# An attention kernel: a planned order of work, and some exponentials computed on VectorE

## The chip, the cores and the metric

The kernel runs on one core of a Trainium2 chip. The metric is the device time of one execution in microseconds; lower is better. The core's engines each run their own queue in order: TensorE (PE in the profile; PEld is its weight load), VectorE (DVE), ScalarE (ACT), GpSimd (POOL) and SyncE (SP), which here issues the transfers between HBM and the core's memory SBUF. TensorE writes to PSUM, eight banks of 2 KB in each partition.

## The reference

Plain attention over 8 batches and 8 heads, 512 queries and keys, 64 dimensions, in fp32:

```python
scale = 1.0 / np.sqrt(q.shape[-1])
scores = np.einsum('bhqd,bhkd->bhqk', q, k) * scale
scores = scores - scores.max(axis=-1, keepdims=True)
attn = np.exp(scores)
attn = attn / attn.sum(axis=-1, keepdims=True)
return np.einsum('bhqk,bhkd->bhqd', attn, v).astype(np.float32)
```

The inputs are normal random numbers. The kernel does not subtract the maximum: it takes the exponential of the scaled scores, and the sum by which it divides comes out of the last product as a 65th column.

## The kernel before

**Tiles.** Two heads make a pair; there are 32 pairs, g = 0 to 31. A pair's queries, keys and values are loaded by SyncE as three tiles of 128 x 512 fp32 (`load`, line 79), cast to fp16 by GpSimd (`cast_v` line 88, `cast_qk` line 95), and queries and keys are turned by TensorE, four 128 x 128 transposes each (`transposes`, line 108), into a PSUM tile that VectorE copies to SBUF (line 109). After that the two heads of a pair lie one above the other, 64 partitions each.

**Scores.** A score block is one chunk of 128 keys of one head against all 512 queries: one matmul with 64 partitions in (line 118). Two blocks make a group, m = 0 to 128; the last two groups have one block each. For most pairs a group has the same chunk of both heads, so a pair has four groups, one for each chunk. A group's scores fill two PSUM banks, `st`, of which there are three pairs; ScalarE reads all 1024 columns and writes the exponentials to SBUF as fp16, `pt` (line 126).

**Values.** When a head's four blocks have their exponentials, 16 small matmuls multiply them with the values, four for each of four parts of the queries (`values`, line 158). The values have a column of ones, so the 65th column of `o` is the sum. VectorE takes its reciprocal (line 136) and multiplies (line 137); that is `normalise`. SyncE stores the pair once both its heads are done.

**Order.** The order on every engine is that of the program text (`manual_schedule`). It is written out by hand: `fill[m]` (lines 229 to 240) lists which transposes and which value products come behind the scores of group m. The values of a head come some six groups behind its scores. Each product's evacuation by VectorE stands right behind it. At the first group of each pair, loads for six pairs ahead and casts for three and two pairs ahead are issued. PSUM outside `st` has two banks: `ps_o` for the products, `ps_t` for the transposes, each with one buffer.

**Head.** `first_loads` and `first_transposes` bring pair 0 in by halves and end with the scores of groups 0 and 1.

Of the kernel before, what the change touches and what calls it, by code (L numbers as in the profile page):

```python
# [7 lines left out]

FP32 = mybir.dt.float32
FP16 = mybir.dt.float16  # L10

EXP = mybir.ActivationFunctionType.Exp
AluOp = mybir.AluOpType


@with_exitstack
def kernel(
# [7 lines left out]
    nc = tc.nc  # L25
# [34 lines left out]
    zeros = cpool.tile([P, S], FP16, name="zeros")  # L60
# [5 lines left out]
    blocks = {}  # L66
    os = {}
    obs = {}

    def source(src, g):  # L70
        b, h = g // ppb, 2 * (g % ppb)
# [26 lines left out]
            )  # L98
        qkp[g] = t

    def transposes(g, n, pool=ps_t, tag="tp"):
        if g >= NP:
            return
        if n == 1:
            tqk[g] = tpool.tile([P, 2, S], FP16, tag="tqk", name=f"tqk_{g}")
        tp = pool.tile([P, NI, P], FP16, tag=tag, name=f"tp_{g}_{n}")
        for i in range(NI):
            nc.tensor.transpose(tp[:, i, :], qkp[g][:, n, i, :], ident)  # L108
        nc.vector.tensor_copy(out=tqk[g][:, n, :], in_=tp.rearrange("p i c -> p (i c)"))  # L109

    def scores(m):
        grp = groups[m]
        size = len(grp)
        st = ps_st.tile([P, 2, S], FP32, tag="st", name=f"st_{m}")
        pt = ppool.tile([P, 2, S], FP16, tag="pt", name=f"pt_{m}")
        for x, (g, c, h) in enumerate(grp):
            po = 64 * h
            nc.tensor.matmul(  # L118
                st[:, x, :],
                tqk[g][po : po + 64, 1, c * P : (c + 1) * P],  # L120
                tqk[g][po : po + 64, 0, :],
                start=True,
                stop=True,
            )
            blocks[(g, c, h)] = pt[:, x, :]
        nc.scalar.activation(  # L126
            out=pt[:, 0:size, :], in_=st[:, 0:size, :], func=EXP, scale=scale
        )

    def normalise(g, h):  # L130
        o = os.pop((g, h))
        if h == 0:
# [3 lines left out]
        nc.vector.reciprocal(out=rc[:, :, :], in_=o[:, :, D : D + 1])  # L136
        nc.vector.tensor_tensor(  # L137
            out=ob[:, h],
            in0=o[:, :, 0:D],
            in1=rc[:, :, :].broadcast_to([P, NI, D]),  # L140
            op=AluOp.mult,
        )
        if g == LAST:
            nc.sync.dma_start(out=source(out, g)[:, h], in_=ob[:, h])
        elif h == 1:
            nc.sync.dma_start(out=source(out, g), in_=ob[:, :, :, :])

    def values(g, h, part):


        last = g == LAST and h == 1
        if part == 0:
            pool, tag = (ps_t, "tp") if g >= LAST - 1 and h == 1 else (ps_o, "o")
            os[(g, h)] = pool.tile([P, NI, D + 1], FP32, tag=tag, name=f"o_{g}_{h}")
        o = os[(g, h)]
        for x in range(NI):
            c, qc = (part, x) if last else (x, part)
            nc.tensor.matmul(  # L158
                o[:, qc, :],
                blocks[(g, c, h)][:, qc * P : (qc + 1) * P],  # L160
                vps[g % NV][:, h, c, :],
                start=(c == 0 and (qc == 0 or not last)),
                stop=(c == NI - 1),
                skip_group_check=last,
            )
        if part == NI - 1:
            normalise(g, h)

    def first_loads():
        tk = load_tile(0, "k")  # L170
        tq = load_tile(0, "q")
# [4 lines left out]
    def first_transposes():  # L176
        tk, tq = raw[0]["k"], raw[0]["q"]
        tqk[0] = tpool.tile([P, 2, S], FP16, tag="tqk", name="tqk_0")
        halves = []
        for h in range(2):  # L180
            t = cpool.tile([P, 2, NI, P], FP16, name=f"qkp_0_{h}")
            nc.gpsimd.memset(t[:, :, :, 64 * (1 - h) : 64 * (1 - h) + 64], 0.0)
            halves.append(t)
        for h in range(2):
            t, s = halves[h], slice(64 * h, 64 * h + 64)
            if h == 0:
                nc.vector.tensor_copy(out=t[:, 1, 0:2, s], in_=tk[:, h, 0:2])  # L187
                nc.vector.tensor_copy(out=t[:, 0, 0:2, s], in_=tq[:, h, 0:2])
                nc.scalar.copy(t[:, 0, 2:4, s], tq[:, h, 2:4])  # L189
                nc.gpsimd.tensor_copy(out=t[:, 1, 2:4, s], in_=tk[:, h, 2:4])  # L190
# [3 lines left out]
        pk = ps_t.tile([P, NI, P], FP16, tag="tp", name="tp_0_k_0")  # L194
        pq = ps_o.tile([P, NI, P], FP16, tag="o", name="tp_0_q_0")
        pk2 = ps_st.tile([P, 2, P], FP16, tag="st", name="tp_0_k2_0")

        def transpose(dst, h, n, i):
            nc.tensor.transpose(dst, halves[h][:, n, i, :], ident)  # L199

        def evacuate(h, n, c0, c1, src):
            s = slice(64 * h, 64 * h + 64)
            nc.vector.tensor_copy(  # L203
                out=tqk[0][s, n, P * c0 : P * c1], in_=src[s].rearrange("p i c -> p (i c)")
            )
# [10 lines left out]
        pk = ps_t.tile([P, NI, P], FP16, tag="tp", name="tp_0_k_1")  # L216
# [4 lines left out]
        pq = ps_o.tile([P, NI, P], FP16, tag="o", name="tp_0_q_1")  # L221
# [7 lines left out]
    fill = [[] for _ in range(M)]  # L229
    for g in range(1, NP):  # L230
        kq = {1: (3, 3), 2: (4, 5)}.get(g, (4 * g - 5, 4 * g - 3))
        fill[kq[0]].append((transposes, (g, 1)))
        fill[kq[1]].append((transposes, (g, 0, ps_o, "o") if g == 1 else (g, 0)))
    for g in range(NP):
        for h in range(2):
            m = 4 * g + 6 + 2 * h
            if (g, h) == (LAST - 1, 1):
                m -= 1
            m = min(m, M - 1)
            fill[m] += [(values, (g, h, part)) for part in range(NI)]  # L240

    with tc.manual_schedule():
        first_loads()
        load(1, "kq")
        load(0, "v")
        for g in range(2, 6):
            load(g, "kq")
            load(g - 1, "v")
        nc.vector.memset(zeros[:, :], 0.0)  # L249
        make_identity(nc, ident)  # L250
        for n in range(NV):
            nc.gpsimd.memset(vps[n][:, :, :, D : D + 1], 1.0)
# [8 lines left out]
        for m in range(M):  # L261
            g, x = divmod(m, 4)
            if x == 0:
                load(g + 6, "kq")
                if g + 5 < NP:
                    load(g + 5, "v")
                cast_qk(g + 3)
                if g + 2 < NP:
                    cast_v(g + 2)
            if m >= 2:  # L270
                scores(m)
            for what, args in fill[m]:
                what(*args)


# [28 lines left out]
```

## Time and profile before

| | |
|---|---|
| median of 3 runs | 129.64 us (129.14 to 130.58) |
| the profiled execution | 129.37 us |
| its span, first to last instruction | 127.5 us |
| ScalarE busy | 119.1 us, 93% |
| TensorE busy | 111.7 us, 88% |
| VectorE busy | 67.5 us, 53% |
| GpSimd busy | 58.3 us, 46% |

Busy shares are of the span. TensorE's matmuls are pipelined and their ends are modelled, so its share does not say how near it is to its limit. A line of a group reads: line, engine, operation, tile written and tile read, their shapes, how many; busy time of all and the mean of one in ns; the engine's idle time ahead of them and what ended it. ScalarE's instructions overlap, so the mean of one is longer than its share of the busy time. In the timeline, times are the start and the length in us.

### The profile page before, as it was taken

The page shows a single profiled execution, that of the slowest core. Times are in us where ns is not written, and L with a number is a line of the kernel's source. Part 1 is how long each engine was busy: PE and PEld are TensorE (multiplying, and loading weights), DVE is VectorE, ACT ScalarE, POOL GpSimd, SP SyncE. Part 2 cuts the span into 40 slices and gives each one's busy share as a digit, 9 for nine tenths or more (in the row PEclk, how much of TensorE's full clock was granted, in tenths as well). Part 3 has the DMA queues.
Part 4 walks back from the last instruction along what each step waited for, and adds up shares of the span by engine and source line. Part 5 has one row for each costly group of instructions (what it writes and reads, how often), then busy time and mean ns, then how long its engine had stood idle before and what let it go on. Part 6 is the DMA issues. An engine that isn't in the chain of part 4 may idle for free.

```text
span 127.5 us, 4004 instructions
## 1 busy us (share of the span) xinstructions
PE 111.7 (88%) x1550; PEld 69.6 (55%) x1550; DVE 67.5 (53%) x198; ACT 119.1 (93%) x131; POOL 58.3 (46%) x111
## 2 busy tenths in 40 slices
PE   6989989889988998898889888988898899888980
PEld 2435656656565655565556555655566565655450
DVE  0535654565456555645665565556555654565161
ACT  4199999999999999999999999999999999999970
POOL 5487858655555533345554333555543347000000
PEclk9999999999999999999999999999999999999996
DMA  3999999999999999988989979989899522222042
GB/s 132 270 352 351 349 351 349 378 370 379 381 348 299 344 373 372 339 272 276 296 248 345 290 249 299 317 275 278 295 306 291 165 85 82 87 82 82 21 133 98
DMA packets 34883, 33.82 MB, mean 265 GB/s; under 512 B 2096, under 2 KB 34864, under 8 KB 34864
## 3 DMA queue, kind: packets, MB, share of 16 engines
q1 hardware_dynamic: 34576, 33.30, 80.6%
q8 instruction: 12, 0.20, 0.7%
q10 hardware_dynamic: 288, 0.26, 0.6%
q14 instruction: 7, 0.06, 0.2%
HBM read 25.17 MB, written 8.39 MB: 263 GB/s over the span
## 4 chain that ended last, share of the span: by engine, by line
ACT 67%; issue 20%; PE 9%; DVE 1%
ACT pt L126 67%; PE st L118 3%; PE o L158 2%; PE warm L255 2%; PE tp L108 1%; PE tp_k L199 1%; PE tp_q L199 0%; DVE ob L137 0%; DVE zeros L249 0%; DVE rc L136 0%
## 5 line engine op out<-in xcount | busy, mean ns | idle before, releaser
L126 ACT ACTIVATE pt<-st 128x1024 f16<-128x1024 f32 x129 | 117.5, 1729 | 2.6 <-PE st L118 2.6
L118 PE MATMUL st<-tqk 64*128 64x512 f16 x256 | 52.0, 384 | 10.7 <-ACT pt L126 10.0
L158 PEld LDWEIGHTS <-pt 128*128 128x128 f16 x1024 | 36.0, 98 | 15.0 <-DVE tqk L109 12.5
L158 PE MATMUL o<-vp,pt 128*128 128x65 f16 x1024 | 43.8, 194 | 0.2 <-ACT pt L126 0.2
L95 POOL CAST qkp<-k 128x512 f16<-128x512 f32 x31 | 19.0, 613 | 44.6 <-issue 34.8
L136 DVE RECIPROCAL rc<-o 128x4 f32<-128x4 f32 x64 | 11.7, 182 | 47.1 <-PE o L158 47.1
L118 PEld LDWEIGHTS <-tqk 64*128 64x128 f16 x256 | 17.4, 93 | 21.3 <-issue 9.5
L137 DVE TENSOR_TENSOR ob<-o,rc 128x256 f32<-128x256 f32 x64 | 27.2, 424 | 2.2
L109 DVE COPY tqk<-tp 128x512 f16<-128x512 f16 x62 | 26.2, 425 | 3.3 <-PE tp L108 2.7
L108 PE MATMUL tp<-ident,qkp 128*128 128x128 f16 x248 | 24.4, 222 | 0.2 <-POOL vp L88 0.2
L108 PEld LDWEIGHTS <-qkp 128*128 128x128 f16 x248 | 14.1, 97 | 14.2 <-issue 7.8
L88 POOL CAST vp<-v 128x512 f16<-128x512 f32 x32 | 19.7, 616 | 1.2
L95 POOL CAST qkp<-q 128x512 f16<-128x512 f32 x31 | 19.0, 614 | 1.4 <-DMA q<-in_q_dram 0.9
L255 PE MATMUL warm<-zeros 128*128 128x512 f16 x6 | 2.7, 630 | 1.2 <-DVE zeros L249 1.2
L189 ACT ACT_TABLE_LOAD x1 | 1.3, 1283 | 1.7 <-PEq L288 1.7
L199 PEld LDWEIGHTS <-qkp 128*128 128x128 f16 x16 | 1.3, 124 | 1.5 <-issue 1.5
L255 PEld LDWEIGHTS <-zeros 128*128 128x128 f16 x6 | 0.7, 138 | 2.3 <-DVE zeros L249 1.2
L187 DVE CAST qkp<-k 128x128 f16<-128x128 f32 x1 | 0.2, 227 | 2.3 <-DMA k<-in_k_dram 2.3
L203 DVE COPY tqk<-tp_q 64x512 f16<-64x512 f16 x2 | 0.8, 422 | 0.9 <-PE tp_q L199 0.7
L199 PE MATMUL tp_k<-ident,qkp 128*128 128x128 f16 x8 | 1.2, 305 | 0.0
L203 DVE COPY tqk<-tp_k 64x256 f16<-64x256 f16 (+1 forms) x3 | 1.0, 328 | 0.4 <-PE tp_k L199 0.3
L199 PE MATMUL tp_q<-ident,qkp 128*128 128x128 f16 x8 | 1.0, 266 | 0.0
(14 smaller groups left out, 4.2 us busy)
## 6 DMA issues: line engine op xcount, KB each, us to landing
v<-in_v_dram SPq DMA_DIRECT2D x32, 256.0 KB, 5.4
k<-in_k_dram SPq DMA_DIRECT2D x31, 256.0 KB, 5.1
q<-in_q_dram SPq DMA_DIRECT2D x31, 256.0 KB, 5.3
out_dram<-ob SPq DMA_DIRECT2D x31, 256.0 KB, 3.7
k<-in_k_dram ACTq DMA_DIRECT2D x2, 128.0 KB, 2.8
q<-in_q_dram SPq DMA_DIRECT2D x2, 128.0 KB, 2.6
out_dram<-ob SPq DMA_DIRECT2D x2, 128.0 KB, 1.7
```

Source lines behind the costliest of these rows:

```text
L88: nc.gpsimd.tensor_copy(out=vps[g % NV][:, :, :, 0:D], in_=raw[g]["v"][:, :, :, :])
L95: nc.gpsimd.tensor_copy(out=t[:, n].rearrange("p i (h d) -> p h i d", h=2), in_=raw[g][name][:, :, :, :],)
L108: nc.tensor.transpose(tp[:, i, :], qkp[g][:, n, i, :], ident)
L109: nc.vector.tensor_copy(out=tqk[g][:, n, :], in_=tp.rearrange("p i c -> p (i c)"))
L118: nc.tensor.matmul(st[:, x, :], tqk[g][po : po + 64, 1, c * P : (c + 1) * P], tqk[g][po : po + 64, 0, :], start=True, stop=True,)
L126: nc.scalar.activation(out=pt[:, 0:size, :], in_=st[:, 0:size, :], func=EXP, scale=scale)
L136: nc.vector.reciprocal(out=rc[:, :, :], in_=o[:, :, D : D + 1])
L137: nc.vector.tensor_tensor(out=ob[:, h], in0=o[:, :, 0:D], in1=rc[:, :, :].broadcast_to([P, NI, D]), op=AluOp.mult,)
L158: nc.tensor.matmul(o[:, qc, :], blocks[(g, c, h)][:, qc * P : (qc + 1) * P], vps[g % NV][:, h, c, :], start=(c == 0 and (qc == 0 or not la ...
L199: nc.tensor.transpose(dst, halves[h][:, n, i, :], ident)
L203: nc.vector.tensor_copy(out=tqk[0][s, n, P * c0 : P * c1], in_=src[s].rearrange("p i c -> p (i c)"))
L255: nc.tensor.matmul(warm[:, 0, :], zeros[:, 0:P], zeros[:, :], start=True, stop=True)
```

## The change

**A planner in place of the written list.** `Plan` steps through time in 5 ns and keeps a time for TensorE, ScalarE and VectorE each, with constants for what things cost (an exponential of a full group 853 + 51 ns, the slot of a group's scores 216, a unit of transposes 224, a unit of values 130, the copy of a pair's transposes 700, a normalisation 640, and latencies between engines). At each step it decides what TensorE and VectorE do next: a group's scores if a score buffer is free and either the next is free too or ScalarE's lead is below 1.1 us; else a unit of transposes or values for which a bank is free. The list of these decisions is the order of the program, on all engines. It also decides for itself when values and transposes come, and on VectorE an evacuation no longer stands right behind its product.

**Exponentials on VectorE.** While no such group is in work, a group with m % 4 = 1 of the pairs 2 to 24 is given to VectorE. It turns the scores into a fixed point number in one instruction (`raise_`: 1024 columns of fp32 from PSUM, written as 32-bit integers; with that the score buffer is free), and then in ten passes over SBUF (`pass_`) makes the exponential: two instructions over 1024 words take out the mantissa and the exponent bits, and four steps of a quartic over the mantissa follow, each as two instructions over 512 columns with two tensors in; the last multiplies with the exponent and writes fp16. A pass comes only if no evacuation that is already known of is due within 390 ns. The next group is given to VectorE only when all ten passes are done.

**What comes with it.** Transposes of queries and keys of a pair share one PSUM bank and one copy of 1024 columns. Products and transposes draw on one pool of two banks, `ps_x`. The exponentials have 36 buffers rather than 12, with three more for VectorE's groups, and the values 12 rather than 6, since a pair may wait longer for its products. The loads and casts of a pair are still issued at its first group, and `feed(0)` ahead of the loop.

```diff
+class Plan:
+    SLOT, EXP, EXP_DONE, EXP_FIXED = 216, 853, 1085, 51
+    INTO, OUT_OF = 95, 105
+    T_UNIT, V_UNIT = 224, 130
+    TO_ACT, TO_DVE, TO_PE = 275, 210, 60
+    COPY, NORM = 700, 640
+    RAISE, PASS, LATE = 1210, 690, 300
...
+    def issue(self, t):
+        m, grp = self.m, self.groups[self.m]
+        g = grp[0][0]
+        heads = [b[2] for b in grp]
+        slots = 1 if len(set(heads)) == 2 else len(grp)
+        on_dve = (
+            self.share
+            and not self.poly
+            and not self.raises
+            and 2 <= g < self.pairs - 7
+            and m % 4 == 1
+        )
+        self.note(t, "scores", m, on_dve)
+        t += (0 if self.tiled else self.INTO) + self.SLOT * slots
+        self.tiled = True
+        if on_dve:
+            self.raises.append((t + self.TO_DVE, m))
+        else:
+            n = len(grp)
+            begin = max(self.act, t + self.TO_ACT)
+            self.act = begin + self.EXP * n // 2 + self.EXP_FIXED
+            self.done[m] = self.exps[m] = self.act + self.EXP_DONE - self.EXP - self.EXP_FIXED
...
+    def step_pe(self, t):
+        if self.m < len(self.groups):
+            now = t >= self.free(self.m)
+            more = self.m + 1 < len(self.groups) and t >= self.free(self.m + 1)
+            slack = self.act - t
+            if now and (more or slack < 1100):
+                return self.issue(t)
+            soon = self.free(self.m)
+            if not now and slack < 1300 and soon < t + 150:
+                return
+        else:
+            now = False
+        if not self.fill(t) and now:
+            self.issue(t)
+
+    def step_dve(self, t):
+        if self.raises and self.raises[0][0] <= t:
+            ready, m = self.raises.pop(0)
+            self.note(t, "raise", m)
+            self.dve = t + self.RAISE
+            self.done[m] = self.dve + self.TO_PE
+            self.poly = [(m, s) for s in range(10)]
+            return
+        if self.evacs and self.evacs[0][0] <= t:
+            ready, what, n = self.evacs.pop(0)
...
+        coming = [x[0] for x in self.raises + self.evacs]
+        if self.poly and min(coming, default=1e9) > t + self.PASS - self.LATE:
+            m, s = self.poly.pop(0)
+            self.note(t, "pass", m, s)
+            self.dve = t + self.PASS
+            if s == 9:
+                self.exps[m] = self.dve + self.TO_PE
...
-    ppool = ctx.enter_context(tc.tile_pool(name="pt", bufs=12))
+    ppool = ctx.enter_context(tc.tile_pool(name="pt", bufs=36))
+    dpool = ctx.enter_context(tc.tile_pool(name="pd", bufs=3))
+    wpool = ctx.enter_context(tc.tile_pool(name="work", bufs=1))
...
-    ps_o = ctx.enter_context(tc.tile_pool(name="ps_o", bufs=1, space=bass.MemoryType.PSUM))
-    ps_t = ctx.enter_context(tc.tile_pool(name="ps_t", bufs=1, space=bass.MemoryType.PSUM))
-
-    NV = 6
+    ps_x = ctx.enter_context(tc.tile_pool(name="ps_x", bufs=2, space=bass.MemoryType.PSUM))
+
+    NV = 12
...
+    def raise_(m):
+        r = raised[m]
+        r["z"] = wpool.tile([P, 2, S], U32, tag="z", name=f"z_{m}")
+        nc.vector.tensor_scalar(
+            out=r["z"][:, :, :],
+            in0=r["st"][:, :, :],
+            scalar1=scale * 1.4426950408889634 * 2.0**23,
+            scalar2=(127 + SHIFT) * 2.0**23,
+            op0=AluOp.mult,
+            op1=AluOp.add,
+        )
+
+    def pass_(m, s):
...
+        n, x = divmod(s - 2, 2)
+        mant = r["m"][:, x, :].bitcast(FP32)
+        nc.vector.scalar_tensor_tensor(
+            out=r["pt"][:, x, :] if n == 3 else r["y"][:, x, :],
+            in0=mant if n == 0 else r["y"][:, x, :],
+            scalar=QUARTIC[n],
+            in1=r["e"][:, x, :].bitcast(FP32) if n == 3 else mant,
+            op0=AluOp.add,
+            op1=AluOp.mult,
+        )
...
+        feed(0)
+        for what, *args in Plan(groups, NP, 2, True).run():
+            if what == "scores":
+                m, on_dve = args
+                g, x = divmod(m, 4)
+                if x == 0 and g < NP:
+                    feed(g)
+                scores(m, on_dve)
+            elif what == "unit":
+                (kind, *args), part = args
+                if kind == "t":
+                    transposes(args[0], part)
+                else:
+                    values(*args, part)
+            elif what == "evac":
+                kind, *args = args[0]
+                (copy if kind == "t" else normalise)(*args)
+            elif what == "raise":
+                raise_(*args)
+            else:
+                pass_(*args)
```

More of the change, by code (lines that the diff above doesn't have):

```diff
@@ L68 @@
     obs = {}
+    raised = {}
     def source(src, g):
@@ L99, in cast_qk, with transposes, copy, scores @@
         qkp[g] = t
[L101 to L104, printed above, removed]
+    def transposes(g, n):
+        if n == 0:
             tqk[g] = tpool.tile([P, 2, S], FP16, tag="tqk", name=f"tqk_{g}")
-        tp = pool.tile([P, NI, P], FP16, tag=tag, name=f"tp_{g}_{n}")
+            tps[g] = ps_x.tile([P, 2, NI, P], FP16, tag="x", name=f"tp_{g}")
         for i in range(NI):
-            nc.tensor.transpose(tp[:, i, :], qkp[g][:, n, i, :], ident)
-        nc.vector.tensor_copy(out=tqk[g][:, n, :], in_=tp.rearrange("p i c -> p (i c)"))
-    def scores(m):
+            nc.tensor.transpose(tps[g][:, n, i, :], qkp[g][:, n, i, :], ident)
+    def copy(g):
+        nc.vector.tensor_copy(
+            out=tqk[g][:, :, :], in_=tps.pop(g).rearrange("p n i c -> p n (i c)")
+        )
+    def scores(m, on_dve=False):
         grp = groups[m]
@@ L114, in scores @@
         st = ps_st.tile([P, 2, S], FP32, tag="st", name=f"st_{m}")
-        pt = ppool.tile([P, 2, S], FP16, tag="pt", name=f"pt_{m}")
+        pool, tag = (dpool, "pd") if on_dve else (ppool, "pt")
+        pt = pool.tile([P, 2, S], FP16, tag=tag, name=f"pt_{m}")
         for x, (g, c, h) in enumerate(grp):
@@ L125, in scores @@
             blocks[(g, c, h)] = pt[:, x, :]
+        if on_dve:
+            raised[m] = {"st": st, "pt": pt}
+            return
         nc.scalar.activation(
@@ L144, in normalise @@
             nc.sync.dma_start(out=source(out, g)[:, h], in_=ob[:, h])
-        elif h == 1:
+        elif not first:
             nc.sync.dma_start(out=source(out, g), in_=ob[:, :, :, :])
@@ L152, in values @@
         if part == 0:
-            pool, tag = (ps_t, "tp") if g >= LAST - 1 and h == 1 else (ps_o, "o")
-            os[(g, h)] = pool.tile([P, NI, D + 1], FP32, tag=tag, name=f"o_{g}_{h}")
+            os[(g, h)] = ps_x.tile([P, NI, D + 1], FP32, tag="x", name=f"o_{g}_{h}")
         o = os[(g, h)]
@@ L165, in values @@
             )
-        if part == NI - 1:
-            normalise(g, h)
     def first_loads():
@@ L225, in first_transposes, with feed @@
         scores(1)
[L229 to L240, printed above, removed]
+    def feed(g):
+        load(g + 6, "kq")
+        if g + 5 < NP:
+            load(g + 5, "v")
+        cast_qk(g + 3)
+        if g + 2 < NP:
+            cast_v(g + 2)
     with tc.manual_schedule():
@@ L260 @@
         cast_v(1)
[L261 to L273, printed above, removed]
+        feed(0)
[17 more added lines that the diff above has]
+                raise_(*args)
+            else:
+                pass_(*args)
 _INS = ['q', 'k', 'v']
```

134 lines of the change are left out of this document (129 added, 5 removed).

## The prediction

> **What bounds the kernel now.** I read the page's busy shares and groups first, then the groups by shape, the waits, the chain that ended last, and the timeline of one steady stretch, of the head and of the tail.
>
> ```profile
> span 127.5 us, 4004 instructions
> PE 111.7 (88%) x1550; PEld 69.6 (55%) x1550; DVE 67.5 (53%) x198; ACT 119.1 (93%) x131; POOL 58.3 (46%) x111
> ```
> ```profile
> 6.11 117.50 ACT L126 ACTIVATE pt<-st 128x1024 f16<-128x1024 f32 x129 [2.58 <-PE st L118]
> ```
> ```profile
> L126 ACT ACTIVATE pt<-st 128x1024 f16<-128x1024 f32 x127 | 116.5, 1736 | 2.6 <-PE st L118 2.6
> L126 ACT ACTIVATE pt<-st 128x512 f16<-128x512 f32 x2 | 1.9, 1274 | 0.0
> ```
> ```profile
> PE st L118 <- ACT pt L126: 10.0, 56, 0.5
> ```
>
> ScalarE runs its 129 exponentials in one unbroken piece from 6.11 to 123.61 us; its one idle stretch is the 2.6 us before the first. The 127 full ones fill 116.5 us, 0.917 each. TensorE waits for ScalarE to give a score buffer back (10.0 us in 56 waits), not the other way round. So 117.5 us of ScalarE plus head and tail is the time. How much of 0.917 is ScalarE's own pace the chain shows:
>
> ```profile
> 98.68 0.64 ACT pt L126
> 113.13 0.85 ACT pt L126
> ```
>
> These are exponentials 16 apart: 14.45 us, 0.903 each. At that pace 127 would take 114.7 us, so 1.8 us of the 116.5 is scores that came a little late.
>
> The profiled execution took 129.37 us: 127.5 of span and 1.87 outside it. The median of the runs is 129.64, 0.27 above it; I add that at the end.
>
> **ScalarE's part: what is removed.** A group on VectorE takes one full exponential away: 0.917 us at the kernel's mean pace. The number of groups follows from the planner's rule: the next group is taken only when the last one's ten passes are all done, only at m % 4 = 1, only for pairs 2 to 24, so for m from 9 to 97. By its own constants a group costs VectorE 1.21 + 10 x 0.69 = 8.11 us, and a pair costs it 0.70 + 2 x 0.64 = 1.98 of the 3.62 us that four exponentials take. 1.64 us are free in a pair, so a group takes 4.9 pairs, some 20 groups of scores; but in 20 groups ScalarE has only 19 to do, so VectorE's share comes up a little short and the step is 20 or, a miss, 24. Steps of 20 give m = 9, 29, 49, 69, 89, five groups; 20, 24, 24 give 9, 29, 53, 77, four. The first step is the easier, because the two heads held up by the group in work need no evacuation before it is done. I take four and keep five as the other end: 4 x 0.917 = 3.7 us removed (4.6 with five).
>
> **VectorE's part: what is added.** No instruction of these forms is in the trace; the nearest rows:
>
> ```profile
> L137 DVE TENSOR_TENSOR ob<-o,rc 128x256 f32<-128x256 f32 x64 | 27.2, 424 | 2.2
> L136 DVE RECIPROCAL rc<-o 128x4 f32<-128x4 f32 x64 | 11.7, 182 | 47.1 <-PE o L158 47.1
> L109 DVE COPY tqk<-tp 128x512 f16<-128x512 f16 x62 | 26.2, 425 | 3.3 <-PE tp L108 2.7
> L203 DVE COPY tqk<-tp_k 64x256 f16<-64x256 f16 x2 | 0.6, 278 | 0.3 <-PE tp_k L199 0.3
> L203 DVE COPY tqk<-tp_k 64x512 f16<-64x512 f16 x1 | 0.4, 427 | 0.0
> ```
>
> From 4 to 256 fp32 elements the time goes from 182 to 424 ns, 0.96 an element; from 256 to 512 fp16 elements from 278 to 427, 0.58 an element. The raise (1024 fp32 from PSUM) at the slow pace: 424 + 768 x 0.96 = 1.16 us. Each of eight half passes (512 fp32, two tensors in): 424 + 256 x 0.96 = 0.67. Each of the two bitwise passes (1024 words, one tensor in, SBUF to SBUF): 427 + 512 x 0.58 = 0.72 at the quick pace, 1.16 at the slow one. I take the quick, because of the first of these three rows: 128 fp32 elements from SBUF took 0.23 us where the slow line gives 424 - 128 x 0.96 = 0.30.
>
> ```profile
> 3.45 0.23 DVE L187 CAST qkp<-k 128x128 f16<-128x128 f32 x1 [2.32 <-DMA k<-in_k_dram]
> 3.48 0.34 POOL L190 CAST qkp<-k 128x128 f16<-128x128 f32 x1 [1.04 <-DMA k<-in_k_dram]
> 3.59 0.31 DVE L188 CAST qkp<-q 128x128 f16<-128x128 f32 x1
> ```
>
> The group is then 1.16 + 2 x 0.72 + 8 x 0.67 = 7.96 us, 8.8 with slow bitwise passes. A dependent neighbour on VectorE starts some 0.03 us later (the first two rows of the timeline below: 60.48 + 0.18, then 60.70); eleven of those make it 8.3. That is what the planner counts with, 8.11, within 0.2.
>
> The same three rows hold the main doubt. The second VectorE cast has the first one's shape but took 0.31 us instead of 0.23. It began inside GpSimd's cast and ended 0.08 us behind its end (3.48 + 0.34 = 3.82; 3.59 + 0.31 = 3.90): it looks as if it stood until GpSimd was through. In the steady stretch VectorE reads PSUM all the time, and its means stand at 424 and 425. The new passes read SBUF only. GpSimd's casts run at:
>
> ```profile
> 60.00:70.00 10.00, 9.14 (x139) 5.90 (x136) 5.48 (x17) 10.00 (x13) 4.91 (x9) 1.00 0.93 296
> ```
> ```profile
> 60.48 0.18 DVE L136 RECIPROCAL rc<-o 128x4 f32<-128x4 f32 x1 [0.76 <-PE o L158]
> 60.70 0.42 DVE L137 TENSOR_TENSOR ob<-o,rc 128x256 f32<-128x256 f32 x1
> 61.22 0.61 POOL L95 CAST qkp<-k 128x512 f16<-128x512 f32 x1 [1.94 <-issue]
> 61.78 0.61 POOL L95 CAST qkp<-q 128x512 f16<-128x512 f32 x1
> ```
>
> In these ten microseconds GpSimd is busy for 4.91 (fifth engine column), in casts of 0.61. A pass that starts at a random moment finds a cast running with chance 0.49 and waits half of one, 0.31: 0.15 a pass, 1.5 us a group. Below it the bound is nothing (only the two bitwise passes, of the same one-input kind as the cast row, wait: 0.3 us), above it half a cast at every pass, 3.1 us.
>
> The Trainium skill, "SBUF — State Buffer", section "SBUF: two separate sides", has a rule for this that speaks against the change: VectorE and GpSimd take a shared pair of SBUF ports as an exclusive lock for a whole instruction, and a VectorE instruction in a two-port mode or with two SBUF inputs needs it. By that rule all ten passes can wait, by the cast row alone only two; the late end of the second cast agrees with the rule, and for two inputs no run so far shows it.
>
> **What becomes of a late VectorE.** Its order is fixed, so an evacuation behind a late pass is late too, the unit of TensorE that needs the PSUM bank waits, and the scores queued behind that unit wait with it. ScalarE feels only what exceeds its lead: the planner lets scores go from 1.1 us of lead down, and three buffers hold at most two exponentials in hand, 1.8; I take 1.45. Late per group: 1.5 of GpSimd and the 0.3 of gaps, 1.8; 0.35 us comes through. Beside it the raised group holds one of three score buffers for 1.16 us and the wait for VectorE, so for about two exponentials ScalarE lives on two buffers. I put 0.15 on that (bounds 0 and 0.5). Together 0.5 a group, 2.0 us for four.
>
> **The modelled order itself.** One copy of 1024 replaces two of 512: 427 + 512 x 0.58 = 0.73 for 0.85, 0.13 us of VectorE a pair, off the path. TensorE's instructions stay what they were; it has room:
>
> ```profile
> 60.38 0.39 PE L118 MATMUL st<-tqk 64*128 64x512 f16 x2
> 60.70 0.40 PE L108 MATMUL tp<-ident,qkp 128*128 128x128 f16 x4
> 61.02 0.09 PEld L118 LDWEIGHTS <-tqk 64*128 64x128 f16 x1
> 61.27 0.39 PE L118 MATMUL st<-tqk 64*128 64x512 f16 x2 [0.17 <-ACT pt L126]
> 61.59 0.68 PE L158 MATMUL o<-vp,pt 128*128 128x65 f16 x16
> 62.21 0.39 PE L118 MATMUL st<-tqk 64*128 64x512 f16 x2
> ```
>
> Two groups and their fill take 1.83 us, and from 61.02 to 61.27 TensorE waits: 1.58 of 1.83 is work. Four groups then cost 3.16 us, 19.0 in 24, where ScalarE takes 23 x 0.903 = 20.8. The scores that came late cost 1.8 us; an order that prefers scores when the lead is short can win between nothing and all of it. I take half, 0.9. The opposite, more late scores from one pair of shared banks, is in the stalls above.
>
> Head and tail I take at nothing. Ahead, six more small memsets on GpSimd (0.3 us for the six of now) fall into the 1.04 us that it idles before its cast at 3.48; without that cover they would delay the first exponential by 0.3. Behind, pairs from 25 on have no raised group, and this end stays:
>
> ```profile
> 123.67 0.30 PE L158 MATMUL o<-vp,pt 128*128 128x65 f16 x4 [0.20 <-ACT pt L126]
> 124.22 0.42 DVE L137 TENSOR_TENSOR ob<-o,rc 128x256 f32<-128x256 f32 x1
> ```
>
> ```profile
> DMA  3999999999999999988989979989899522222042
> ```
>
> The bound behind is one held-up head more at the end, 0.62 us of TensorE (61.59 to 62.21) and the 0.64 of its normalisation. SP's queue gets the held pair's output where the planner puts it, and loads queue behind it; the loads are done by the 32nd of 40 slices, about 100 us (the transfers' share falls from 9 to 2 tenths), with 25 us to spare, so I put no price on that.
>
> **Sum.** 129.37 - 3.7 - 0.9 + 2.0 = 126.8; with 0.27 to the median, 127.0 us.
>
> **Rivals.**
> - VectorE waits for nothing and five groups fit: 129.64 - 4.6 - 0.9 = 124.1. For it: TensorE's room and the planner's constants, which agree with the rows. Against: the 0.31 us cast, and VectorE with no room left while a group is in work (8.3 of 1.6 us a pair).
> - The stalls eat what is removed: 0.92 a group come through, and with little or nothing from the order it is 128.7 to 129.6. So too if the planner places one or two groups only: 129.64 - 0.9 or 1.8, less half of it for stalls.
> - Slower: each pass waits half a cast, because a waiting cast starts at the very moment a pass ends and the next pass stands behind it; GpSimd's casts come in rows of three without a gap (61.22, 61.78), which is for it. Against it: an evacuation between two passes lets a cast run by its side. Late per group 3.1 + 0.3 = 3.4, less 1.45 of lead, plus 0.15: 2.1 us come through for 0.92 removed. 4 x 1.2 = 4.8 slower, less 0.9: 129.64 + 3.9 = 133.5. It decides from 2.2 us of lateness a group on (1.45 + 0.92 - 0.15), about 0.2 us a pass; by the Trainium skill's lock (same section) waits of that size are open to all ten passes, not to two.
>
> **How the numbers follow.** The forecast, 125.5 to 128.3, has 0.40; the better case, about 124.1, 0.13; no change 0.22; slower 0.25. About 1% is what a measurement of this kernel can tell from no change, so faster ends at 128.3 and slower begins at 130.9: 0.53, 0.22, 0.25. The range is 124.2 to 133.0: it leaves out some 0.06 of the better case and half of the slower one, 0.13. The forecast's own range is 125.5 to 128.3.
>
> **What would show it.** Exponentials: 125 on ScalarE rather than 129 and a piece of about 113 us plus stalls (117.5 - 3.7 - 0.9). Raise at 1.16, passes at 0.67 and 0.72 where GpSimd is idle; longer passes that end just behind a cast would show the wait. ScalarE gaps before L126 released by TensorE, and those TensorE waits released by VectorE, would be the price; if they lie within a group's ten passes the mechanism is right. Wrong it would be if ScalarE idles over 1 us a group, if passes never stretch beside casts, or if the number of groups is not four or five.

## The result

The changed kernel took 125.45 us (median; before 129.43 in the same runs): 0.967 of the time before, 95% interval 0.961 to 0.973. The prediction was 127.0 us, faster. In a second comparison the ratio was 0.976 (0.973 to 0.979), 125.93 us against 129.06. The profile that came with the first timing is of a disturbed execution (128.07 us), so the lines below are those of an execution of the same kernel that took 125.48 us.

Its page, span and busy shares:

```profile
span 123.6 us, 4005 instructions
PE 110.1 (89%) x1550; PEld 66.1 (53%) x1550; DVE 93.4 (76%) x211; ACT 115.5 (93%) x127; POOL 67.6 (55%) x117
```

ScalarE in its timeline (start, length, operation, count):

```profile
5.82 113.88 ACT L313 ACTIVATE pt<-st 128x1024 f16<-128x1024 f32 x125 [2.17 <-PE st L302]
```

125 exponentials rather than 129, so four groups went to VectorE, and again one piece without a gap, now 113.88 us long rather than 117.50. The 3.62 us between them are the whole gain inside the piece, 0.905 for each exponential removed. In both traces the ends of the full exponentials follow each other by 0.917 us (median; before, all but the last within 0.002 of it). Four of those are 3.67; the missing 0.05 is one end that came late at 10.5 us, ahead of the first group on VectorE. The span fell by 3.9; the rest is a head 0.3 us shorter (5.82 for 6.11), and heads differ by more than that in the runs below (5.45 to 6.28).

VectorE's new instructions, in the groups by shape (busy time, mean of one in ns):

```profile
L362 DVE SCALAR_TENSOR_TENSOR y<-y,m 128x512 f32<-128x512 f32 x16 | 12.4, 777 | 0.0
L362 DVE SCALAR_TENSOR_TENSOR y<-m 128x512 f32<-128x512 f32 x8 | 6.9, 866 | 0.0
L362 DVE SCALAR_TENSOR_TENSOR pt<-y,e 128x512 f16<-128x512 f32 x8 | 6.5, 807 | 0.0
L327 DVE TENSOR_SCALAR z<-st 128x1024 uint32<-128x1024 f32 x4 | 4.9, 1219 | 0.1
L340 DVE TENSOR_SCALAR m<-z 128x1024 uint32<-128x1024 uint32 x4 | 3.6, 896 | 0.0
L351 DVE TENSOR_SCALAR e<-z 128x1024 uint32<-128x1024 uint32 x4 | 3.5, 865 | 0.0
```

The raise takes 1.22 us. The ten passes of four groups together take 32.9 us, 8.2 a group, and their means lie well above what a pass takes when it is quick. Why, the timeline of the third group shows, VectorE and GpSimd side by side:

```profile
59.17 1.22 DVE L327 TENSOR_SCALAR z<-st 128x1024 uint32<-128x1024 f32 x1
...
65.02 1.01 DVE L340 TENSOR_SCALAR m<-z 128x1024 uint32<-128x1024 uint32 x1
65.96 0.68 DVE L351 TENSOR_SCALAR e<-z 128x1024 uint32<-128x1024 uint32 x1
66.55 0.17 DVE L378 RECIPROCAL rc<-o 128x4 f32<-128x4 f32 x1
66.76 0.42 DVE L379 TENSOR_TENSOR ob<-o,rc 128x256 f32<-128x256 f32 x1
67.10 1.11 DVE L362 SCALAR_TENSOR_TENSOR y<-m 128x512 f32<-128x512 f32 x1
```
```profile
64.88 0.62 POOL L269 CAST vp<-v 128x512 f16<-128x512 f32 x1
66.31 0.80 POOL L276 CAST qkp<-k 128x512 f16<-128x512 f32 x1 [0.81 <-PE o L399]
67.06 0.61 POOL L276 CAST qkp<-q 128x512 f16<-128x512 f32 x1
67.62 1.06 POOL L269 CAST vp<-v 128x512 f16<-128x512 f32 x1
```

The first bitwise pass starts at 65.02, inside a cast that ends at 65.50, and takes 1.01 us; the second starts at 65.96 with GpSimd idle and takes 0.68. The two-input pass at 67.10, behind a cast that runs to 67.67, takes 1.11. It goes both ways: the cast at 67.62 meets that pass and takes 1.06 instead of 0.61. The reciprocal and the multiplication between them read the product from PSUM and do not change (0.17 and 0.42).

### The profile page after: what moved, and what is told of

The parts are those of the page before. It is cut to its first block, busy times and chain, and to the rows that moved or that the text cites. A ratio compares the mean times of both kernels' runs of the same rounds, so it can differ in the third digit from the quotient of the medians.

```text
span 126.3 us, 4005 instructions
## 1 busy us (share of the span) xinstructions
PE 113.3 (90%) x1550; PEld 67.9 (54%) x1550; DVE 93.5 (74%) x211; ACT 115.7 (92%) x127; POOL 66.9 (53%) x117
## 4 chain that ended last, share of the span: by engine, by line
ACT 41%; PE 38%; issue 15%; DMA 2%; DVE 1%; POOL 0%; ACTq 0%
ACT pt L313 41%; PE st L302 16%; PE o L399 14%; PE tp L287 6%; DMA k<-in_k_dram 2%; PE tp_k L437 1%; PE tp_q L437 1%; DVE ob L379 1%; DVE rc L378 0%; POOL qkp L428 0%; ACTq L313 0%
## 5 line engine op out<-in xcount | busy, mean ns | idle before, releaser
L313 ACT ACTIVATE pt<-st 128x1024 f16<-128x1024 f32 (+1 forms) x125 | 114.2, 1339 | 4.5 <-PE st L302 4.5
L399 PE MATMUL o<-vp,pt 128*128 128x65 f16 x1024 | 52.0, 196 | 6.5 <-ACT pt L313 5.7
L290 DVE COPY tqk<-tp 128x1024 f16<-128x1024 f16 x31 | 21.2, 684 | 7.0 <-PE tp L287 7.0
L302 PEld LDWEIGHTS <-tqk 64*128 64x128 f16 x256 | 13.0, 94 | 15.9 <-issue 8.9
L287 PE MATMUL tp<-ident,qkp 128*128 128x128 f16 x248 | 20.1, 225 | 0.6 <-DVE ob L379 0.4
L362 DVE SCALAR_TENSOR_TENSOR y<-y,m 128x512 f32<-128x512 f32 x16 | 12.5, 779 | 0.0
L362 DVE SCALAR_TENSOR_TENSOR y<-m 128x512 f32<-128x512 f32 x8 | 7.1, 890 | 0.0
L362 DVE SCALAR_TENSOR_TENSOR pt<-y,e 128x512 f16<-128x512 f32 x8 | 6.1, 764 | 0.0
L327 DVE TENSOR_SCALAR z<-st 128x1024 uint32<-128x1024 f32 x4 | 4.9, 1220 | 0.1
L351 DVE TENSOR_SCALAR e<-z 128x1024 uint32<-128x1024 uint32 x4 | 3.9, 969 | 0.0
```

The lines of the kernel that those rows point to most:

```text
L287: nc.tensor.transpose(tps[g][:, n, i, :], qkp[g][:, n, i, :], ident)
L290: nc.vector.tensor_copy(out=tqk[g][:, :, :], in_=tps.pop(g).rearrange("p n i c -> p n (i c)"))
L302: nc.tensor.matmul(st[:, x, :], tqk[g][po : po + 64, 1, c * P : (c + 1) * P], tqk[g][po : po + 64, 0, :], start=True, stop=True,)
L313: nc.scalar.activation(out=pt[:, 0:size, :], in_=st[:, 0:size, :], func=EXP, scale=scale)
L327: nc.vector.tensor_scalar(out=r["z"][:, :, :], in0=r["st"][:, :, :], scalar1=scale * 1.4426950408889634 * 2.0**23, scalar2=(127 + SHIFT) * ...
L362: nc.vector.scalar_tensor_tensor(out=r["pt"][:, x, :] if n == 3 else r["y"][:, x, :], in0=mant if n == 0 else r["y"][:, x, :], scalar=QUAR ...
```

## The experiments

**The order without the groups.** The planner's `share` is set to false.

```diff
-        for what, *args in Plan(groups, NP, 2, True).run():
+        for what, *args in Plan(groups, NP, 2, False).run():
```

> The planned order with no group on VectorE. Theory A (the raised groups carry the gain and cost nothing beside: four times 0.92 us, and the order is neutral): 129.0 to 129.5 us. Theory B (the prediction's sum: the order wins 0.9 us and each raised group gives back 0.5): 128.5 us. Theory C (the order itself wins 2 us or more and the raised groups only half of what they remove): 127.5 us or less.

129.23 us, 1.001 of the kernel before (0.999 to 1.003). Its ScalarE line and its wait:

```profile
5.97 117.50 ACT L313 ACTIVATE pt<-st 128x1024 f16<-128x1024 f32 x129 [2.50 <-PE st L302]
```
```profile
PE st L302 <- ACT pt L313: 0.7, 2, 0.5
```

The piece has the same 117.50 us as before, to the last digit. The order did change how TensorE is fed: it waited 10.0 us for score buffers before and 0.7 here. ScalarE gained nothing by that. The order is worth nothing that this interval could show, as theory A had it.

**The changed kernel again, beside it.** No edit.

> The changed kernel as it is, beside the others on one chip. Every theory: about 125.5 us, four exponentials fewer on ScalarE (125), no idle stretch of ScalarE after its first exponential that is as long as 0.1 us if the lateness of VectorE is covered; idle stretches of 0.3 to 0.5 us a raised group if the prediction's stall term holds.

125.93 us, the lines above. ScalarE is idle nowhere after its first exponential, so nothing of the lateness reached it as a gap.

**Three groups.** The last pair for groups is moved forward.

```diff
-            and 2 <= g < self.pairs - 7
+            and 2 <= g < self.pairs - 16
```

> Only the first two groups (m = 9, 33) go to VectorE. If each group is worth one exponential, 0.905 us, with nothing lost: 127.4 us, halfway between the planned order alone (129.2) and the changed kernel (125.6). If the groups' worth falls off with their number or place: away from halfway by more than 0.5 us.

126.48 us, 0.976 (0.968 to 0.984). The expectation had miscounted: pairs up to 15 include m = 61, and the trace has 126 exponentials, so three groups. With that its own rate, 129.2 - 3 x 0.905 = 126.5, gives what was measured.

**Five groups, from pair 1 or from pair 3.** In the first the planner may begin at pair 1 and a pass may delay an evacuation that is known of by 600 ns; in the second it begins at pair 3, at odd m, with 700 ns, and may go on to pair 29.

```diff
-    RAISE, PASS, LATE = 1210, 690, 300
+    RAISE, PASS, LATE = 1210, 690, 600
...
-            and 2 <= g < self.pairs - 7
+            and 1 <= g < self.pairs - 7
```

> The planner may begin at pair 1 and may let a pass delay a known evacuation by 600 rather than 300 ns; it then places five groups (m = 5, 25, 49, 73, 97). If a raised group is worth 0.92 us and its lateness is covered: 124.5 us. If VectorE's room is used up by the tighter spacing: 125.5 us or more, with ScalarE idle for the difference.

```diff
-    RAISE, PASS, LATE = 1210, 690, 300
+    RAISE, PASS, LATE = 1210, 690, 700
...
-            and 2 <= g < self.pairs - 7
-            and m % 4 == 1
+            and 3 <= g < self.pairs - 2
+            and m % 2 == 1
```

> Five groups, the first at m = 13 after the dense casts of the head (13, 33, 55, 77, 99), a pass may delay a known evacuation by 700 ns. If the early place of the first group cost the other five-group order its gain: 124.6 to 125.0 us with no idle time of ScalarE. If tighter spacing itself costs it: 125.5 us or more, with idle time spread over all groups.

The early one took 125.74 us, 0.973 (0.968 to 0.978), no better than four groups; the later one 124.57, 0.960 (0.946 to 0.974), the fastest kernel of this study. ScalarE's lines of the early one, then the line of the later one:

```profile
5.83 13.86 ACT L313 ACTIVATE pt<-st 128x1024 f16<-128x1024 f32 x15 [2.34 <-PE st L302]
19.86 2.86 ACT L313 ACTIVATE pt<-st 128x1024 f16<-128x1024 f32 x3 [0.17 <-PE st L302]
22.88 4.69 ACT L313 ACTIVATE pt<-st 128x1024 f16<-128x1024 f32 x5 [0.17 <-PE st L302]
27.82 91.84 ACT L313 ACTIVATE pt<-st 128x1024 f16<-128x1024 f32 x101 [0.26 <-PE st L302]
```
```profile
5.89 112.94 ACT L313 ACTIVATE pt<-st 128x1024 f16<-128x1024 f32 x124 [2.23 <-PE st L302]
```

Both have 124 exponentials. The early one stood 0.6 us in three gaps between 19 and 28 us, two in the later passes of its first group and one just before its second raise (by the ends of its exponentials they cost 0.9); the later one has no gap and a piece 0.94 us shorter than with four groups. The two differ in place, spacing and the delay allowed, so it is the whole order that is shown better, and the early place as its cause is only likely.

**Five groups with wide steps.** The quartic's steps are four instructions over 1024 columns, counted by the planner at 1215 ns each (`dve = t + 1215` for them), 600 ns of delay, pairs 3 to 27.

```diff
-        n, x = divmod(s - 2, 2)
-        mant = r["m"][:, x, :].bitcast(FP32)
+        n = s - 2
+        mant = r["m"][:, :, :].bitcast(FP32)
         nc.vector.scalar_tensor_tensor(
-            out=r["pt"][:, x, :] if n == 3 else r["y"][:, x, :],
+            out=r["pt"][:, :, :] if n == 3 else r["y"][:, :, :],
...
```

> The quartic's steps as four instructions over 1024 columns in place of eight over 512 (4 x 1.21 for 8 x 0.68: 0.6 us less of VectorE a group), the planner knowing; five groups at m = 13, 33, 53, 73, 93. If a group is worth 0.905 us as long as VectorE has room: 124.6 us, as the five groups from m = 13 with half passes. If an evacuation behind a 1.2 us instruction comes too late: 125.5 us or more with idle time of ScalarE inside the groups.

124.88 us, 0.965 (0.961 to 0.969): five groups again, ScalarE's piece 112.92 us without a gap. VectorE is busy 97.9 us rather than the 101.5 of the later five with half steps, but nothing waits for that. It allows 600 ns as the early five do, so that allowance alone does not make the gaps.

**No casts beside the passes.** `cast_qk` and `cast_v` do nothing from pair 4 on; pair 3's queries and keys and the first four values tiles are used instead.

```diff
     def cast_v(g):
+        if g >= 4:
+            return
...
+        if g >= 4:
+            qkp[g] = qkp[3]
+            return
...
-                vps[g % NV][:, h, c, :],
+                vps[g % 4][:, h, c, :],
```

> GpSimd casts only the first four pairs; the later ones use pair 3's queries and keys and the values of pairs 0 to 3, so most of the output is another one and only the time counts. From the second raised group on no cast runs beside the passes. If casts make passes wait, all ten passes of those groups are 0.67 to 0.69 us (two-input ones as well as bitwise ones) and the group's lateness falls by about 1.45 us. If that lateness is covered by lead and idle time in the changed kernel, the time stays within 0.5 us of 125.5; if it comes through in part, the time falls by up to 3 x 1.45 = 4 us.

125.66 us, 0.969 (0.961 to 0.977). The passes, with the least, median and greatest ns of one:

```profile
L367 DVE SCALAR_TENSOR_TENSOR y<-y,m x16: 680/682/683, 23.2 to 101.1; 128x512 f32<-128x512 f32 x16
L367 DVE SCALAR_TENSOR_TENSOR y<-m x8: 680/682/686, 19.0 to 93.8; 128x512 f32<-128x512 f32 x8
```

In the changed kernel the same line reads:

```profile
L362 DVE SCALAR_TENSOR_TENSOR y<-y,m x16: 679/714/1104, 23.1 to 100.8; 128x512 f32<-128x512 f32 x16
L362 DVE SCALAR_TENSOR_TENSOR y<-m x8: 679/794/1107, 19.0 to 94.0; 128x512 f32<-128x512 f32 x8
```

Without casts every pass takes 0.68 us, bitwise ones too (means 683 and 685 ns), with them up to 1.11. So the waits come from the casts. At 0.68 the ten passes of four groups would take 27.3 us, and they took 32.9: 5.6 us, 1.4 a group in the mean (0.6 to 2.1 in single groups), was waiting. Of the 40 passes 20 took more than 0.70, by 0.28 in the mean. And the time is the same without it. This is the plainest answer to the prediction's main doubt: the wait is there and nothing waits for it.

The Trainium skill, "SBUF — State Buffer", section "SBUF: two separate sides", says that the port pair shared by VectorE and GpSimd is held for a whole instruction, also by a VectorE instruction with two SBUF inputs when GpSimd's reads SBUF. The two-input passes at up to 1.11 beside casts and 0.68 without them agree.

Where the wait goes, the two traces show side by side: TensorE, ScalarE and VectorE have the same order in both, and the one without casts runs 0.31 us behind from its head on. In the third group, first with casts, then without:

```profile
69.27 0.91 DVE L362 SCALAR_TENSOR_TENSOR y<-m 128x512 f32<-128x512 f32 x1
70.10 0.17 DVE L378 RECIPROCAL rc<-o 128x4 f32<-128x4 f32 x1
```
```profile
69.07 0.68 DVE L367 SCALAR_TENSOR_TENSOR y<-m 128x512 f32<-128x512 f32 x1
70.21 0.18 DVE L383 RECIPROCAL rc<-o 128x4 f32<-128x4 f32 x1 [0.46 <-PE o L404]
```

With the 0.31 taken off, the pass begins 0.51 us later with casts and is 0.23 longer, so it ends 0.74 late; the reciprocal begins only 0.20 late, because the 0.46 us for which VectorE stood before it without casts are gone. Compared in this way instruction by instruction, 0.74 is the most that VectorE is late anywhere behind the head, and in each group it is back within 0.02 before the last pass. While the ten passes run it stands idle 2.2 to 3.0 us a group without casts and 0.9 to 1.7 with them. The scores hardly notice: behind the head all but four groups of scores end at the same time before their exponential in both traces, to 0.05 us, and those four come at most 0.16 later with casts. So VectorE's idle time takes up the wait, ahead of TensorE's scores, and ScalarE's lead is hardly drawn on.

**How much lateness is covered.** Five kernels repeat an instruction with the same result, unknown to the planner: the raise twice, the last quartic step twice, both bitwise passes twice, the first and the last step twice, both bitwise passes three times. Each edit has this form:

```diff
+        for _ in range(2):
             nc.vector.tensor_scalar(
                 out=r["z"][:, :, :],
...
-        nc.vector.scalar_tensor_tensor(
+        for _ in range(2 if n == 3 else 1):
+            nc.vector.scalar_tensor_tensor(
```

> The raise is done twice with the same result: the score buffer is held 1.22 us longer and VectorE is 1.22 us later, unknown to the planner, at the start of each group. The prediction put 0.15 us a group on the held buffer. If neither the buffer nor the lateness reaches ScalarE: 125.5 to 126 us. If two buffers are too few for longer: ScalarE idles up to 1.2 us a group right behind the raise, up to 5 us more, 130 us.

> The two passes of the quartic's last step done twice each: 1.4 to 1.7 us more a group, one pass at a time between evacuations, at the end of the group. If idle time between evacuations takes it up: under 1 us more, 125.5 to 126.5 us. If lateness adds up over the group and has no lead left at its end: 4 x 1.5 = 6 us more, 131.5 us.

> Each bitwise pass done twice, unknown to the planner: 1.4 to 2.0 us more of VectorE a raised group, in or near one block. The tripled passes (3.6 us more a group) cost 16 us, all of it and more. If the changed kernel's lead is already used up: half of that, 7 to 8 us, 133 us. If there is still some lead left, of L a group: less by 4 L; at L = 1 us about 129 us, at L of 1.8 us or more 125.5 to 126 us.

> The four passes of the quartic's first and last step are done twice each with the same result, without the planner's knowing: 4 x 0.68 to 0.85 us = 2.7 to 3.4 us more of VectorE in each raised group, as much as in the run with tripled bitwise passes, but spread over the group instead of in two blocks. If all lateness beyond that of the changed kernel comes through (the lead is used up already): about 11 to 14 us more, 137 to 140 us. If only blocks of several microseconds without an evacuation hurt, and idle time between evacuations absorbs the rest: under 4 us more, 129 us or less.

> Each of the two bitwise passes is done three times, with the same result, and the planner does not know of it: 4 x 0.69 to 1.0 us, 2.8 to 4 us more of lateness on VectorE in each raised group. If only ScalarE's lead of about 1.45 us covers lateness, as the prediction had it, nearly all of it comes through: 8 to 14 us more, 134 to 139 us. If VectorE's own idle time between evacuations absorbs it, less than half of it comes through: 125.5 to 130 us, with the smaller figure if the idle time lies within the group's ten passes.

In the table, VectorE's additional work is its busy time above the changed kernel's 93.4 us, and the additional time is that above 125.7 (between its two medians), each over four groups. The kernels ran on two chips, on which the kernel before took 129.1 to 129.6 us, so 0.1 us a group means nothing. Where the executions lie far apart, their range stands in brackets or in place of a median.

| kernel | VectorE more, a group | time | ratio to before (95%) | time more, a group |
|---|---|---|---|---|
| no casts | -1.1 us | 125.7 us | 0.969 (0.961 to 0.977) | 0.0 us |
| raise twice | 1.15 | 127.3 | 0.983 (0.977 to 0.988) | 0.4 |
| last step twice | 1.7 | 128.4 | 0.997 (0.991 to 1.003) | 0.7 |
| bitwise twice | 2.15 | 131.4 to 135.1 | no interval | 1.4 to 2.3 |
| first and last step twice | 3.35 | 131.9 (131.6 to 135.7) | 1.017 (1.002 to 1.033) | 1.6 (1.5 to 2.5) |
| bitwise three times | 3.65 | 141.5 (141.2 to 144.9) | 1.096 (1.092 to 1.101) | 4.0 (3.9 to 4.8) |

The changed kernel sits near the edge of what is covered. Its own 1.4 us of waiting costs nothing; another 1.15 us already lets about a third through, and 1.7 two fifths. Three expectations were missed: the one for the last step twice had under 1 us or 6 in all, and it was 2.7; the one for the first and last step twice had under 4 or 11 to 14, and it was 6; the bitwise passes three times cost 16, where 14 was the most. Of the raise twice, 1.6 us of up to 5, it is not separated whether the buffer held longer or VectorE's lateness costs.

The cost is not spread evenly over the groups either. In the last step twice, 1.5 of the 1.9 us for which ScalarE stands idle are one gap at the second raise, which comes 2.0 us later than in the changed kernel (34.05 there):

```profile
30.69 1.70 DVE L363 SCALAR_TENSOR_TENSOR pt<-y,e 128x512 f16<-128x512 f32 x2
32.86 2.12 DVE L363 SCALAR_TENSOR_TENSOR pt<-y,e 128x512 f16<-128x512 f32 x2
36.05 1.22 DVE L327 TENSOR_SCALAR z<-st 128x1024 uint32<-128x1024 f32 x1
```
```profile
36.63 48.82 ACT L313 ACTIVATE pt<-st 128x1024 f16<-128x1024 f32 x53 [1.51 <-PE st L302]
```

From the first of these rows to the raise VectorE has no idle time that could take the lateness up.

Where the lateness comes counts as much as how long it is: 3.35 us of single passes done twice cost 1.5 to 2.5, 3.65 in blocks of bitwise passes cost all of it and more. The blocks also stand at another place, at the start of a group's passes, and length and place were not separated. Of the bitwise passes done twice it is shown only that they are dear; the executions lie too far apart for a figure.

What a block does, the third group of the tripled passes shows (timeline; in brackets the idle time before an instruction and who ended it):

```profile
73.03 3.09 DVE L341 TENSOR_SCALAR m<-z 128x1024 uint32<-128x1024 uint32 x3
...
75.27 0.30 PE L401 MATMUL o<-vp,pt 128*128 128x65 f16 x4
76.04 2.55 DVE L353 TENSOR_SCALAR e<-z 128x1024 uint32<-128x1024 uint32 x3
78.51 0.18 DVE L380 RECIPROCAL rc<-o 128x4 f32<-128x4 f32 x1
78.72 0.42 DVE L381 TENSOR_TENSOR ob<-o,rc 128x256 f32<-128x256 f32 x1
...
79.29 1.01 PE L287 MATMUL tp<-ident,qkp 128*128 128x128 f16 x8 [3.72 <-DVE ob L381]
80.24 1.03 PE L302 MATMUL st<-tqk 64*128 64x512 f16 x4
...
80.95 1.94 ACT L313 ACTIVATE pt<-st 128x1024 f16<-128x1024 f32 x2 [3.72 <-PE st L302]
```
```profile
72.00:78.00 6.00, 3.25 (x47) 1.83 (x44) 5.67 (x8) 5.23 (x6) 3.90 (x6) 1.00 0.81 275
78.00:84.00 6.00, 4.71 (x44) 2.70 (x44) 4.72 (x11) 2.96 (x3) 2.24 (x3) 0.52 0.28 86
```

Six bitwise passes hold VectorE from 73.03 to 78.59. Both banks are full from 75.57 on. TensorE stands 3.72 us before the transposes of line 287, until the normalisation frees a bank; the scores behind them in its queue come no earlier; ScalarE stands 3.72 us too. This is the chain that the prediction described. And there seems to be a surcharge: from 78 to 84 us TensorE's granted clock is 0.52 instead of 1.00 (the second window, first figure behind the five engines), and eight transposes take 1.01 us, which take 0.61 in the changed kernel. ScalarE stands another 0.7 us, in two gaps that end at 84.2 and 85.7 us. That the clock is what makes them is likely, not shown.

## Why the prediction was right, and where its sum was off

The direction, the number of groups and the worth of one were right, and so was the size of the wait that was feared. Two terms were wrong, with opposite signs: 2.0 us for lateness and 0.9 for the order, and both came out at nothing. Without them the sum would have been 129.64 - 3.7 = 125.9, where 125.45 and 125.93 were measured. That 127.0 came as near as it did is in part luck, since 0.9 of the 2.0 cancelled; 125.45 lies just below the forecast's own range, which began at 125.5.

- **ScalarE's part.** Four groups were predicted and came, at 0.917 us each: 3.7 us. Measured: 3.62 in ScalarE's piece. It is linear in the number of groups as far as these times tell: 129.23 us with none, 126.48 with three, 125.45 and 125.93 with four, 124.57 with five, so 0.92 us a group with three, 0.83 to 0.95 with four, 0.93 with five.
- **The steps of the groups.** The trace has raises at about 13, 34, 59 and 84 us: m = 9, 33, 61 and 89, steps of 24, 28 and 28 where the working had 20, 24, 24. Between m = 9 and 97 every equal step of 24 or 28 gives four groups, so that the number held is no proof of the steps. The third group's first pass starts at 65.02, 4.6 us behind the end of the raise at 60.39: VectorE first worked off evacuations. The step had passes begin at once; the spacing came out wider, and that is room.
- **VectorE's part.** Raise 1.16 predicted, 1.22 measured; two-input passes 0.67 and 0.68; bitwise 0.72 and 0.68, so they do run at the quick pace; the single copy of 1024 columns 0.73 and 0.68. The wait for casts: 1.5 us a group predicted from GpSimd's share and half a cast (chance 0.49, 0.31 us), 1.4 measured (20 of 40 passes, 0.28 us), and at bitwise as well as two-input passes. Here the mechanism was right, not only the number.
- **What becomes of a late VectorE** is the step that failed: "0.35 us comes through", with 0.15 for the held buffer, 2.0 us in all. Measured: nothing. It added the waits of a whole group up and set against them ScalarE's lead, 1.45 us, as a fixed sum. But the wait comes in pieces of at most 0.43 us, pass by pass, and VectorE has idle time between them, in which it catches up; the step left that out. Against the kernel without casts it is never more than 0.74 us late, and the idle time before its reciprocals is what shrinks, here with casts and then without:

```profile
DVE rc L378 <- PE o L399: 14.4, 31, 1.7
```
```profile
DVE rc L383 <- PE o L404: 17.9, 37, 1.7
```

  ScalarE's lead was not the cover. Worked out from the ends of the scores (which are modelled) and of the exponentials before them, it is 0.76 to 1.28 us in the steady stretches, and 0.34 to 0.37 for the two groups behind each raised one. So a raised group does take lead away (its scores give ScalarE nothing to do, and its buffer is held), but in the changed kernel not all of it, and the price put on the held buffer was nothing too. The chain itself (bank, unit, scores, exponential) is the one that the tripled passes show.
- **The modelled order** is the other failed step: 0.9 us was to be won from "scores that came a little late", 1.8 us of them. There were none. The pace of 0.903 us was read from the starts of exponentials 16 apart, but starts in this trace run ahead of the work: in the kernel before, one exponential takes from 1019 to 2187 ns in the record, longer and longer where the starts are close. The ends of the full ones are 0.917 us apart all along, as the piece has it (116.5 us for 127), and they stay so in the planned order alone, where TensorE hardly waits for buffers. ScalarE was never waiting, and the page had said so: its only idle time was ahead of the first exponential.
- **The slower rival** is refuted for this kernel, but not far off. Its passes were to wait 0.31 each and waited 0.14. It put the break-even at 2.2 us of lateness a group. With the last step twice, 1.4 + 1.7 = 3.1 us a group, the kernel is no slower than before yet (0.997); in blocks, 1.4 + 3.65 us is slower by 10%. So the point depends on where the lateness falls, and a single figure for it was the wrong form.
- **The better rival** took VectorE to wait for nothing and five groups to fit. The waits are there, but five groups do fit in another order: 124.57 us, where it had 124.1, with 0.9 for the order in it that was not there.
- **The chances.** Faster had 0.53. The sum without the two failed terms would have supported more, since what was removed was certain and what was added lay on engines off the path; the doubt about the lock was sized rightly, and its cover was not.

What stays open: the worth of the early place of a group, whether a block's length or its place makes it dear, and how much of a block's price is the lower clock behind it.

## What to carry to other kernels

Where one engine runs without a gap, its time falls by its own pace for each piece of work that is taken off it, and the question is only whether the engine that takes it over can be late without anyone noticing; repeating an instruction with the same result shows how near that edge is. Compare lateness with the helping engine's own idle time between its other duties, piece by piece, before setting its sum against the lead of the bottleneck. Hand the work over in short pieces between the evacuations: in the tripled passes, lateness in one block stopped the chain of PSUM bank, matmul and next scores at full length. Read an engine's pace from the ends of its instructions or the length of its unbroken piece, not from the distance of their starts.

## What the runs showed of the hardware that was not expected

- The wait between VectorE and GpSimd goes both ways: casts that took 613 to 616 ns in the mean before take 691 to 724 here, and one that met a pass 1.06 us. GpSimd's busy time rose from 58.3 to 67.6 us with the same casts and six more small memsets.
- After 3.7 us without work in mid-kernel TensorE was granted half its clock (0.50 from 78.2 to 85.0 us in the tripled passes). The Trainium skill, "TensorE: Matmul & The Clock Gate", section "Why this matters for your kernels", warns of gaps of over some 3 us between matmuls. This stand agrees, but shorter ones had the same here: 0.51 from 46.0 to 52.9 us around a stand of 2.0 us in the bitwise passes done twice, and 0.50 from 37.0 to 40.4 us around one of 1.34 us in the first and last step done twice. One of 1.35 us, in the last step twice, had not.
- Bitwise operations on 1024 32-bit words took 0.68 us, as long as a two-input instruction over 512: these one-input instructions handled about two words in the time in which the two-input ones handled one.
